# Dilated attention in a three-block network: token order set when queries and keys are evicted, values of two groups reordered through DRAM

## The chip, the cores and the metric

One core of a Trainium2 chip runs the whole program. The metric is the device time of one execution in microseconds. The kernel before was run three times: 3733.88, 3742.0 and 3743.15 us, median 3742.0 us.

## The reference

The network has three blocks of layers over 512 tokens of width 1024. The change lies in the second block, whose attention has twelve heads of 64 in three groups of four. Group 0 looks at neighbouring tokens in blocks of 128. Groups 1 and 2 are dilated by 4: token t belongs to sub-sequence t mod 4, and each of the four sub-sequences of 128 tokens attends only to itself. Cut to what matters, for one group:

```python
def to_sub(t):                       # dilation r, L = S // r
    return t.reshape(B, L, dilation, H, hd).transpose(0, 2, 3, 1, 4)
s = einsum('brhnqd,brhnkd->brhnqk', to_sub(q), windows(to_sub(k))) * hd ** -0.5
s = where(valid, s - slopes * dist, -inf)
p = exp(s - max(s));  l = sum(p)
o = einsum('brhnqk,brhnkd->brhnqd', p, windows(to_sub(v))) / l
```

The three groups are merged by their log-sum-exp. Everything is computed in float32.

## The kernel before

Activations lie with the features on the 128 partitions and the 512 tokens along the free dimension. A float32 product is made from three products of a high and a low part (`mm3`, line 253, and `gemm_tok`, lines 354 to 356): high by high, high by low, low by high. Weights arrive in tiles of 128 x 1024 (512 KB) on SP's queue (line 236) into three buffers `wraw`; ScalarE copies the high part (`whi`, line 369), VectorE takes the difference (`wlo`, line 370).

`gemm` computes features by tokens: the weight block is the stationary operand, the tokens move, 512 columns at a time. 24 matmuls make one output tile `pg`, of which there are two in PSUM, and an `evac` function empties it. `gemm_tok` computes tokens by features, for the values: the stationary operand is 128 tokens of the activations `h`, the weights move, and four output tiles (two `pg`, two `pa`) are filled in turn, 96 matmuls in all for a weight of up to 512 columns.

In the second block `b2_body` runs the product of the convolution branch (12 feature tiles), then `b2_attention`, then further products (`ev_sc` and on). `b2_attention` (line 1531) loops over the three groups. For each, `project(g)` computes two tiles of queries and two of keys with `gemm` and empties them on ScalarE (lines 1545 and 1547), computes the values with `gemm_tok` at 256 columns (line 1550, emptied on ScalarE), and four bias tiles on VectorE (line 1553). Then 16 units follow (`unit`, four blocks j by four heads): a score product (line 834, queries stationary, keys moving), a biased maximum on VectorE (line 837), an exponential on ScalarE (line 838), a transpose on TensorE (line 847), a copy on ScalarE (line 850) and the product with the values (line 854). In group 0 a unit has one or two key blocks (28 in 16 units); in groups 1 and 2 it has one.

The tokens of a dilated block j are every fourth token. `b2_sub` (line 1416) picks them by a view with a step of four elements:

```python
return ap.rearrange("p (l r) -> p r l", r=4)[:, j]
```

This view is used for the stationary tokens of the values of groups 1 and 2, and for both operands of their score products. `b2_merge` (line 1581) uses it again at the end.

Program order and priorities set the order on each engine; it is fixed when the kernel is built. The units belong to a second stream, so that TensorE gets the products of the next `project` between the steps of the units. The depthwise convolution of 31 taps (`b2_conv`, line 1510, VectorE) is emitted with a later priority and fills VectorE beside these stages. Tiles of `s4` (queries, keys, values, bias, outputs) come from 25 buffers; `tmp` of stream "d" has four buffers.

Of the kernel before, what the change touches and what calls it, by code (L numbers as in the profile page):

```python
# [10 lines left out]
F32 = mybir.dt.float32  # L11
# [3 lines left out]
AF = mybir.ActivationFunctionType  # L15
# [4 lines left out]
T = 512  # L20
# [30 lines left out]
class Core:  # L51
# [422 lines left out]
    def ffn(self, h, up, down, conv, end):  # L474


        nc = self.nc
        self.set_rows(h)
        hid = self.parts()
        held = {}  # L480

        def ev(m, ps):
            j = m // 2
            u = ps
            if conv is not None:
                u = self.tmp()
                self.conv_evac(u, ps, lambda i: conv(m * 3 + i), 3)
            if m % 2 == 0:
                s = self.tmp()
                nc.scalar.activation(s, u, AF.Silu)  # L490
                held[j] = s
            else:
                s = held.pop(j)
                nc.vector.tensor_mul(s, s, u)  # L494
                self.split(hid.hi(j), hid.lo(j), s)

        self.gemm(up, h, ev, wide=True)
        evac, after = end()
        self.gemm(down, hid, evac, tail=getattr(evac, "tail", 0))
        with self.stream("b"):  # L500
            return after()
# [911 lines left out]
class Block2:  # L1413


    def b2_sub(self, ap, g, j):
# [2 lines left out]
            return ap[:, j * 128 : j * 128 + 128]  # L1419
        return ap.rearrange("p (l r) -> p r l", r=4)[:, j]  # L1420

    def b2_mixer(self, h, end):
        with self.phase("b2", 25, dict(a=2, b=4, d=4)):
            return self.b2_body(h, end)
# [106 lines left out]
    def b2_attention(self, w, h, at):  # L1531
        nc, a = self.nc, self.a
        ml = self.small([128, 2, 3, 4, 4], tag="ml", bufs=1)
        nm, ls = ml[:, 0], ml[:, 1]
        ob, qs, ks, vs, bs, pos = [], [], [], [], [], {}

        def project(g):
            q, k, v, bias = self.s4(), self.s4(), self.s4([128, 4, 256]), self.s4([128, 4, 256])
            for l, t in ((qs, q), (ks, k), (vs, v), (bs, bias)):
                l.append(t)  # L1540

            def ev(m, ps):
                i = (m - 12) % 4
                if i < 2:
                    nc.scalar.activation(q[:, i], ps, AF.Copy, scale=0.125)
                else:
                    nc.scalar.activation(k[:, i - 2], ps, AF.Copy)

            self.gemm(w, h, ev, 12 + 4 * g, 4)
            self.gemm_tok(a["b2_v"], self.tok(h, lambda x, j: self.b2_sub(x, g, j)), lambda j, ps: nc.scalar.activation(v[:, j], ps, AF.Copy), g * 256, 256)  # L1550
            wd = 256 if g == 0 else 128
            for hd in range(4):
                nc.vector.tensor_scalar(bias[:, hd, :wd], self.c(f"d{g}"), -float(2.0 ** (-8.0 * (4 * g + hd + 1) / 12)), None, ALU.mult)

        def unit(g, j, hd):
            r = slice(hd % 2 * 64, hd % 2 * 64 + 64)
            q, k, v = qs[g][r, hd // 2], ks[g][r, hd // 2], vs[g]
            if g == 0:
                vb = max(j - 1, 0)
                k, bias = k[:, vb * 128 : (j + 1) * 128], bs[g][:, hd, 256 - 128 * (j + 1 - vb) : 256]  # L1560
            else:
                vb, k, bias = j, self.b2_sub(k, g, j), bs[g][:, hd, :128]
            wd = bias.shape[-1]
            p = self.attn_scores(self.b2_sub(q, g, j), k, wd, bias, ls[:, g, j, hd : hd + 1], m=nm[:, g, j, hd : hd + 1])
            yield
            if hd == 0:
                pos[g, j] = self.ps()
                if j == 0:
                    ob.append(self.s4([128, 4, 256]))
            self.attn_pv(pos[g, j][:, hd * 64 : hd * 64 + 64], p, wd, lambda b: v[:, vb + b, hd * 64 : hd * 64 + 64])  # L1570
            if hd == 3:
                nc.scalar.activation(ob[g][:, j], pos.pop((g, j))[:, :256], AF.Copy)

        for g in range(3):
            project(g)
            with self.stream("b"):
                self.pipeline(unit(g, j, hd) for j in range(4) for hd in range(4))
        with self.stream("b"):
            self.b2_merge(ob, nm, ls, at)
# [42 lines left out]
class Block3:  # L1622
# [47 lines left out]
    def b3_body(self, h, end):  # L1670
# [81 lines left out]
        rproj = lambda: proj("b3_rproj", 0, ry, parts)  # L1752
        work = [*qkv, *gates, zs, rproj]
        xs = [run(j, self.rwkv_in, w, h, j) for j in range(2)]
        for j in range(4):
            if 0 < j < 3:
                xs.append(run(j + 1, self.rwkv_in, w, h, j + 1))
            n = B3_FILL[j]
            fill(B3_PACE[j], work[:n])
            del work[:n]  # L1760
            run(j, self.rwkv, xs[j], j, lora, lt, gs, half, oka, ry)
# [371 lines left out]
class Net(Core, Layer0, Layer1, Block2, Block3):  # L2133
# [348 lines left out]
    def run(self, out):  # L2482
        nc, tc, a = self.nc, self.tc, self.a
        self.xd = self.ctx.enter_context(tc.tile_pool(name="xd", bufs=1, space=bass.MemoryType.DRAM)).tile([128, KD, T], F32, name="xd")
        self.gd = self.ctx.enter_context(tc.tile_pool(name="gd", bufs=1, space=bass.MemoryType.DRAM)).tile([128, 16, T], F32, name="gd")
        self.xin = a["xT"]
        self.mod = self.cpool.tile([128, 96], F32, name="mod")
        units = lambda layer, m0, m1: [lambda m=m: self.ada_bg(layer, m) for m in range(m0, m1, 2)]
        ada = [units(0, 16, 40), units(0, 40, 48) + units(1, 0, 40), [], units(1, 40, 48)]
        with self.psum(a=2, b=4):  # L2490
            with tc.tile_pool(name="ada", bufs=1) as self.apool:
                self.scb = self.apool.tile([128, D], F32, name="scb")
                with self.phase("x0", dict(s4=4, sq=2, wa0=WA0), dict(a=3), side="right"):
                    h = self.first_norm()

                for layer in range(2):
                    self.bg.extend(ada[2 * layer])
                    self.bg_per = 1
                    end = self.end_gated(layer, f"l{layer}_post_m", 2, self.ada_norm(f"l{layer}_pre_f", layer, 4, 3), TAIL[layer])
                    h = (self.l1_mixer if layer else self.l0_mixer)(h, end)  # L2500
                    self.bg_flush()
                    self.bg.extend(ada[2 * layer + 1])
                    self.bg_per = FBG
                    if layer == 0:
                        norm = self.ada_norm("l1_pre_m", 1, 1, 0)
                    else:
                        norm = lambda r, x, update, h, half: self.norm_h(r, x, lambda k: self.v("b2_g1", k), None, update, h, half)
                    with self.phase(f"ffn{layer}", 26, dict(d=3, b=2)):
                        h = self.ffn(h, a[f"l{layer}_up"], a[f"l{layer}_down"], None, self.end_gated(layer, f"l{layer}_post_f", 5, norm, TAIL[2 + layer], False))
                    self.bg_flush()  # L2510

            ffn = lambda n, h, end: self.ffn(h, a[f"b{n}_up"], a[f"b{n}_down"], lambda c: self.v(f"b{n}_fw", c), end)
            h = self.b2_mixer(h, self.end_add("b2_g2"))
            with self.phase("ffn2", 26, dict(d=6, b=3)):
                h = ffn(2, h, self.end_block)
        with self.psum(a=3, b=3):
            h = self.b3_mixer(h, self.end_add("b3_g2"))
            with self.phase("ffn3", 26, dict(d=6, b=3)):
                ffn(3, h, lambda: self.end_last(out))
# [23 lines left out]
```

## Time and profile before

| what | value |
|---|---|
| median of three runs | 3742.0 us |
| the profiled execution | 3741.21 us |
| its span in the trace | 3739.4 us |
| mean granted clock of TensorE | 0.975 of full speed |
| TensorE (PE) busy | 3637.7 us, 97% |
| weight loads into TensorE (PEld) | 2956.0 us, 79% |
| VectorE (DVE) busy | 2192.0 us, 59% |
| ScalarE (ACT) busy | 1357.4 us, 36% |

The span is what the trace covers; 1.8 us lie around it. PE is the matmul, PEld the load of the stationary operand, which can run beside the matmul before it. A busy PE says that matmuls were in flight, not that they ran at their best rate, so that the pitch of the matmuls (start to start) and the granted clock have to be read too.

### The profile page before, as it was taken

Reading aid. Unit: us, or ns where it says so; the run is one execution under the profiler, and the core shown is the slowest. Engines: PE = TensorE matmul, PEld = TensorE weight load, DVE = VectorE, ACT = ScalarE, POOL = GpSimd, SP = SyncE. Lnnn points to the kernel's source line nnn. Section 1 sums busy time; section 2 is a strip of 40 time slices with the busy share of each in tenths; the row PEclk is TensorE's granted clock in tenths of the full one; section 3 lists DMA queues with packets and bytes.
Section 4 is the critical chain, followed back from the end, with each engine's and each line's share of the span. In section 5 each row is a group of like instructions: output and inputs, shape, how many; then the busy total and the mean of one; then the engine's idle time right before and its main releaser. Section 6 shows DMA issues by size and latency. Waiting matters only on the chain.

```text
span 3739.4 us, 50867 instructions
## 1 busy us (share of the span) xinstructions
PE 3637.7 (97%) x20496; PEld 2956.0 (79%) x20496; DVE 2192.0 (59%) x3821; ACT 1357.4 (36%) x2197; POOL 242.1 (6%) x216
## 2 busy tenths in 40 slices
PE   6998999999999999999999999999999999999999
PEld 5776888878887788878888888788877777887887
DVE  7866665454377653349519354675466655766752
ACT  5444432334254432323332243443343332333432
POOL 2003100110021200100000010000000000100000
PEclk9999999999999999999979999999999999999999
DMA  6511265533300242323112234223321111052232
GB/s 216 184 46 62 98 208 193 167 108 101 122 28 23 68 158 96 118 90 110 51 40 74 86 103 138 96 96 119 110 83 42 62 63 44 27 186 86 98 116 78
DMA packets 120220, 373.56 MB, mean 100 GB/s; under 512 B 12064, under 2 KB 20256, under 8 KB 119984
## 3 DMA queue, kind: packets, MB, share of 16 engines
q1 hardware_dynamic: 105008, 322.05, 26.4%
q10 hardware_dynamic: 14976, 48.26, 3.8%
q8 instruction: 161, 2.64, 0.3%
q14 instruction: 75, 0.61, 0.1%
HBM read 349.29 MB, written 20.97 MB: 99 GB/s over the span
## 4 chain that ended last, share of the span: by engine, by line
PE 91%; DVE 6%; ACT 1%; issue 1%; DMA 0%; POOL 0%; POOLq 0%; DVEq 0%; ACTq 0%
PE pg L253 67%; PE pa L253 3%; PE pb L854 2%; PE pb L834 1%; PE pb L847 1%; PE pb L1274 1%; DVE wlo L370 1%; PE pa L392 1%; PE pg L1361 1%; PE pb L2275 1%; PE pg L354 1%; PE pa L354 1%; PE pa L355 1%; PE pg L356 1%; PE pg L355 1%
## 5 line engine op out<-in xcount | busy, mean ns | idle before, releaser
L253 PE MATMUL pg<-h,whi 128*128 128x512 f32 (+1 forms) x5584 | 1776.2, 397 | 45.4 <-ACT h L463 14.4
L253 PEld LDWEIGHTS pg<-h,whi 128*128 128x128 f32 x5584 | 1049.1, 191 | 278.2 <-issue 18.7
L253 PE MATMUL pg<-h,wlo 128*128 128x512 f32 (+1 forms) x2792 | 1101.2, 395 | 0.0
L369 ACT ACTIVATE whi<-wraw 128x1024 fp32r<-128x1024 f32 (+3 forms) x540 | 546.9, 1014 | 1351.0 <-PE pg L253 1062.8
L370 DVE TENSOR_TENSOR wlo<-wraw,whi 128x1024 fp32r<-128x1024 f32 (+3 forms) x540 | 638.9, 1184 | 638.6 <-ACT whi L369 636.0
L253 PE MATMUL pg<-s,whi 128*128 128x512 f32 (+1 forms) x2044 | 620.5, 386 | 3.4 <-DVE s L916 2.8
L253 PEld LDWEIGHTS pg<-h,wlo 128*128 128x128 f32 x2792 | 533.5, 191 | 109.7 <-issue 4.2
L253 PEld LDWEIGHTS pg<-s,whi 128*128 128x128 f32 x2044 | 379.9, 189 | 84.1 <-DVE s L916 3.2
L253 PE MATMUL pg<-s,wlo 128*128 128x512 f32 (+1 forms) x1022 | 392.7, 384 | 0.0
L253 PEld LDWEIGHTS pg<-s,wlo 128*128 128x128 f32 x1022 | 192.9, 189 | 38.0
L807 DVE SCALAR_TENSOR_TENSOR td<-td,vec,td 128x511 f32<-128x511 f32 (+1 forms) x188 | 139.9, 747 | 59.8 <-ACT td L803 58.2
L2153 DVE CUSTOM_DVE_ANT_0 wa<-wa,scb,vec 128x1024 f32<-128x1024 f32 x90 | 121.3, 1350 | 65.6 <-DMA wa<-in_l_ada_dram 65.5
L332 DVE TENSOR_TENSOR td<-pg,rows 128x512 f32<-128x512 f32 x130 | 89.3, 688 | 86.1 <-PE pg L253 85.6
L1510 DVE SCALAR_TENSOR_TENSOR s<-s,vec,s 128x504 f32<-128x504 f32 (+25 forms) x180 | 121.5, 731 | 0.4
L854 PEld LDWEIGHTS pb<-s,tb 128*128 128x128 f32 x600 | 86.3, 203 | 31.4 <-DVE tb L852 9.1
L369 ACT ACTIVATE s<-td 128x512 fp32r<-128x512 f32 x94 | 59.3, 631 | 106.8 <-DVE td L494 106.3
L253 PE MATMUL pa<-h,whi 128*128 128x512 f32 (+1 forms) x336 | 95.8, 359 | 0.0
L854 PE MATMUL pb<-s,tb 128*128 128x64 f32 x600 | 92.3, 284 | 3.2 <-DVE tb L852 3.2
L370 DVE TENSOR_TENSOR s<-td,s 128x512 fp32r<-128x512 f32 x94 | 66.9, 712 | 30.7 <-ACT s L369 30.7
L494 DVE TENSOR_TENSOR td<-td,pg 128x512 f32<-128x512 f32 x44 | 30.2, 687 | 75.9 <-PE pg L253 75.8
L253 PEld LDWEIGHTS pa<-h,whi 128*128 128x128 f32 x336 | 61.2, 194 | 8.9 <-issue 0.2
L803 ACT ACTIVATE td<-td,vec 128x512 f32<-128x512 f32 x94 | 66.5, 709 | 4.5 <-DVE td L332 3.1
(804 smaller groups left out, 4145.2 us busy)
## 6 DMA issues: line engine op xcount, KB each, us to landing
wraw<-in_b_in_dram SPq DMA_DIRECT2D x112, 512.0 KB, 3.2
wraw<-in_l_up_dram SPq DMA_DIRECT2D x88, 512.0 KB, 3.2
wraw<-in_b_up_dram SPq DMA_DIRECT2D x88, 512.0 KB, 3.2
wa<-in_l_ada_dram ACTq DMA_DIRECT2D x80, 512.0 KB, 3.2
wraw<-in_l_in_dram SPq DMA_DIRECT2D x51, 512.0 KB, 3.5
wraw<-in_l_down_dram SPq DMA_DIRECT2D x32, 512.0 KB, 3.5
wraw<-in_b_down_dram SPq DMA_DIRECT2D x32, 512.0 KB, 3.5
xd<-s SPq DMA_DIRECT2D x28, 512.0 KB, 2.7
```

The costliest lines, as they stand in the source:

```text
L253: mm = lambda *a, **k: self.nc.tensor.matmul(*a, **k, skip_group_check=True)
L332: self.nc.vector.tensor_mul(y, ps, rows)
L354: nc.tensor.matmul(pss[j][:, :n], xh, wh, start=k == 0, stop=False)
L355: nc.tensor.matmul(pss[j][:, :n], xl, wh, start=False, stop=False)
L356: nc.tensor.matmul(pss[j][:, :n], xh, wl, start=False, stop=k == nk - 1)
L369: i = nc.scalar.activation(hi, src, AF.Copy)
L370: nc.vector.tensor_sub(lo, src, hi.bitcast(F32))
L803: nc.scalar.activation(out, ps, AF.Copy, scale=w(taps - 1))
L807: nc.vector.scalar_tensor_tensor(out[:, s:], ps[:, : T - s], w(taps - 1 - s), out[:, s:], ALU.mult, ALU.add)
L854: nc.tensor.matmul(o, st[:, b * 128 : b * 128 + 128], v(b), start=b == 0, stop=b == nb - 1)
L1510: nc.vector.scalar_tensor_tensor(out[:, s:], x[:, : T - s], tap(30 - s), out[:, s:], ALU.mult, ALU.add)
L2153: nc.vector.tensor_tensor_reduce(w, w, self.scb, 1.0, b, ALU.mult, ALU.add, o)
```

## The change

The values of groups 1 and 2 are computed first, by one `gemm_tok` of 512 columns on the tokens in their natural order. Each of its four output tiles is copied by ScalarE into a `tmp` and written to a DRAM tile `vd` (two groups, 512 tokens, 256 columns), 256 KB at a time, on ScalarE's queue. `project(1)` and `project(2)` no longer compute values: they load their `v` tile from `vd` on SP's queue, 512 KB, so that partition l holds tokens 4l to 4l+3. Queries and keys of groups 1 and 2 are written in the order of the sub-sequences when they are emptied from PSUM: the read of PSUM has the step of four, the tile in SBUF is then contiguous for each block, and the score products read it without a step. Group 0 is as before.

```diff
+    def b2_values(self, h):
+        nc = self.nc
+        def ev(j, ps):
+            t = self.tmp()
+            nc.scalar.activation(t, ps, AF.Copy)
+            nc.scalar.dma_start(self.vd[:, j * 128 : j * 128 + 128].rearrange("g t n -> t g n"), t.rearrange("p (g n) -> p g n", g=2))
+        self.gemm_tok(self.a["b2_v"], self.tok(h), ev, 256, 512)
...
             def ev(m, ps):
                 i = (m - 12) % 4
-                if i < 2:
-                    nc.scalar.activation(q[:, i], ps, AF.Copy, scale=0.125)
-                else:
-                    nc.scalar.activation(k[:, i - 2], ps, AF.Copy)
+                o = (q, k)[i // 2][:, i % 2]
+                if g:
+                    o, ps = o.rearrange("p (r l) -> p r l", r=4), ps.rearrange("p (l r) -> p r l", r=4)
+                nc.scalar.activation(o, ps, AF.Copy, scale=1.0 if i // 2 else 0.125)
             self.gemm(w, h, ev, 12 + 4 * g, 4)
-            self.gemm_tok(a["b2_v"], self.tok(h, lambda x, j: self.b2_sub(x, g, j)), lambda j, ps: nc.scalar.activation(v[:, j], ps, AF.Copy), g * 256, 256)
+            if g:
+                nc.sync.dma_start(v, self.vd[g - 1].rearrange("(l r) n -> l r n", r=4))
+            else:
+                self.gemm_tok(a["b2_v"], self.tok(h), lambda j, ps: nc.scalar.activation(v[:, j], ps, AF.Copy), 0, 256)
...
-                vb, k, bias = j, self.b2_sub(k, g, j), bs[g][:, hd, :128]
+                vb, k, bias = j, k[:, j * 128 : j * 128 + 128], bs[g][:, hd, :128]
             wd = bias.shape[-1]
-            p = self.attn_scores(self.b2_sub(q, g, j), k, wd, bias, ls[:, g, j, hd : hd + 1], m=nm[:, g, j, hd : hd + 1])
+            p = self.attn_scores(q[:, j * 128 : j * 128 + 128], k, wd, bias, ls[:, g, j, hd : hd + 1], m=nm[:, g, j, hd : hd + 1])
...
+        self.b2_values(h)
         for g in range(3):
             project(g)
...
+        self.vd = self.ctx.enter_context(tc.tile_pool(name="vd", bufs=1, space=bass.MemoryType.DRAM)).tile([2, T, 256], F32, name="vd")
```

## Rows read from the trace of the kernel before

**Rows 1.** The page: busy time, and the chain that ended last, by engine.

```profile
PE 3637.7 (97%) x20496; PEld 2956.0 (79%) x20496; DVE 2192.0 (59%) x3821; ACT 1357.4 (36%) x2197; POOL 242.1 (6%) x216
...
PE 91%; DVE 6%; ACT 1%; issue 1%; DMA 0%; POOL 0%; POOLq 0%; DVEq 0%; ACTq 0%
```

**Rows 2.** Busy time by stretch: length, engines (counts), clock, DMA share, GB/s.

```profile
core 0: us, PE busy (x) PEld busy (x) DVE busy (x) ACT busy (x) POOL busy (x), PEclk, DMA share, GB/s
1400.00:1500.00 100.00, 100.00 (x443) 82.81 (x442) 33.83 (x37) 29.60 (x38) 0.00 (x0) 1.00 0.29 97
...
1773.20:1785.00 11.80, 11.80 (x98) 11.55 (x96) 11.80 (x20) 3.47 (x6) 0.00 (x0) 1.00 0.28 90
1785.00:1820.40 35.40, 35.40 (x181) 25.25 (x180) 28.62 (x65) 20.41 (x60) 0.00 (x0) 1.00 0.10 32
...
1827.90:1850.60 22.70, 22.70 (x99) 22.57 (x100) 3.00 (x6) 4.17 (x7) 0.00 (x0) 1.00 0.15 47
```

**Rows 3.** Timeline of PE: first and last of the 96 value matmuls, group 1.

```profile
1827.93 0.28 PE L354 MATMUL pg<-whi,h 128*128 128x256 f32 x1
...
1849.99 0.39 PE L356 MATMUL pa<-wlo,h 128*128 128x256 f32 x1
```

**Rows 4.** Line 355, values: weight loads (ns min/median/max) of groups 0 and 1.

```profile
L355 PEld LDWEIGHTS pg<-whi,h x16: 187/192/192, 1773.3 to 1783.9; 128*128 128x128 f32 x16
...
L355 PEld LDWEIGHTS pg<-whi,h x16: 310/329/329, 1827.9 to 1848.2; 128*128 128x128 f32 x16
```

**Rows 5.** Timeline of PE around a score product of groups 0 and 1.

```profile
1789.39 0.48 PE L834 MATMUL pb<-s,s 64*128 64x128 f32 x2
1789.81 0.33 PE L847 MATMUL pb<-cst,tb 128*128 128x128 f32 x1
...
1854.59 0.83 PE L834 MATMUL pb<-s,s 64*128 64x128 f32 x2
1855.35 0.50 PE L253 MATMUL pg<-h,wlo 128*128 128x512 f32 x1
```

**Rows 6.** Line 834, score products: weight loads of group 0, then of group 1.

```profile
L834 PEld LDWEIGHTS pb<-s,s x32: 182/184/186, 1785.1 to 1813.7; 64*128 64x128 f32 x32
...
L834 PEld LDWEIGHTS pb<-s,s x32: 304/316/328, 1850.3 to 1881.6; 64*128 64x128 f32 x32
```

**Rows 7.** Line 253 alone by stretch: length, PE, PEld (counts), clock, DMA share, GB/s.

```profile
1785.00:1820.40 35.40, 19.68 (x63) 10.84 (x64) 1.00 0.10 32
...
1850.60:1864.30 13.70, 6.37 (x19) 3.25 (x19) 1.00 0.12 39
1864.30:1887.80 23.50, 14.80 (x26) 7.77 (x27) 0.50 0.07 22
...
1922.20:1929.30 7.10, 3.42 (x11) 1.89 (x12) 1.00 0.23 74
1929.30:1960.30 31.00, 17.18 (x28) 8.40 (x28) 0.50 0.05 17
...
1980.00:1992.00 12.00, 10.19 (x24) 6.23 (x23) 0.57 0.28 89
```

**Rows 8.** Line 834 alone, start of group 1's attention: columns as in rows 7.

```profile
1850.70:1864.30 13.60, 6.14 (x18) 3.93 (x16) 1.00 0.12 40
```

**Rows 9.** Eviction of queries (line 1545), then copies without and with step.

```profile
L1545 ACT ACTIVATE s<-pg x6: 574/580/593, 1757.9 to 1889.9; 128x512 f32<-128x512 f32 x6
...
L1594 DVE COPY s<-pb x6: 673/1042/1081, 1960.6 to 1964.8; 4x512 f32<-4x512 f32 x6
```

**Rows 10.** DMA: issue on ScalarE's queue, then transfers through DRAM (us to landing).

```profile
L1718 ACTq DMA_DIRECT2D gd<-td x16: 326/326/336, 2951.7 to 3172.9; - x16
...
s<-xd SPq DMA_DIRECT2D x28, 512.0 KB, 6.0
...
gd<-td ACTq DMA_DIRECT2D x16, 256.0 KB, 2.3
```

**Rows 11.** Timeline of DVE: the last eviction of the product ahead of the attention.

```profile
1752.24 0.68 DVE L1439 TENSOR_TENSOR s<-td,pg 128x512 f32<-128x512 f32 x1
```

## The prediction

> **What bounds the kernel now.** I read the page first: TensorE is busy 97% of the span and carries 91% of the chain that ended last [rows 1], so time is won where TensorE's own work shrinks. But busy is not fast. In the table by stretch a plain 512-column product runs 443 matmuls in 100 us, a pitch of 0.226 us [rows 2]; this is the yardstick. The stretch of the values of group 1 is just as busy, yet it puts 96 matmuls of only 256 columns into 22.3 us (first to last 22.06 us over 95 steps, 0.232 us each) [rows 3]. In that stretch PEld is busy 22.57 of 22.70 us [rows 2]: the weight loads set the pace. They take 329 ns where they read every fourth token and 192 ns where they read neighbours [rows 4]. Third, the score products: a unit of 128 keys holds TensorE 0.76 us in group 1 and 0.42 us in group 0 [rows 5], with weight loads of 316 against 184 ns [rows 6]. Last, the granted clock, by stretch: it is 1.00 (2.4 GHz) throughout the attention of group 0, but falls to 0.50 (1.2 GHz) after 13.7 us in that of group 1 and after 7.1 us in that of group 2, and stays there for 23.5 and 31.0 us [rows 7]. TensorE was never idle there; what differs from group 0 is the stepped operands and one key block per unit instead of up to two.
>
> **The values.** Removed: two stretches like the one in rows 3, 2 x 96 x 0.232 = 44.5 us, all on TensorE, with nothing else in flight. Added: one product of 96 matmuls of 512 columns on neighbouring tokens. Its weight loads are the 192 ns kind and hide behind a 512-column matmul, so the pitch is the yardstick's: 96 x 0.226 = 21.7 us. **Gain 22.8 us.** The weight bytes are the same, six tiles of 512 KB.
>
> The Trainium skill (SBUF — State Buffer, Specifications (TRN2), row on cachelines) says that SBUF reads are fast when at least two hits fall into a 16-byte line, so that a step of four float32 pays on every element. By that rule the contiguous load runs at its full rate; the 329 against 192 ns above agree in direction, and the sum uses the rows alone.
>
> **The scores.** 32 units of groups 1 and 2 lose 0.76 - 0.42 = 0.34 us each, 10.9 us if the clock is full.
>
> **The clock.** I count it together with the scores, from whole stretches. Attention of group 1 lasts 13.7 + 23.5 = 37.2 us and holds 45 plain matmuls (10.2 us at the yardstick), so its 16 units cost 27.0 us. Group 2 lasts 38.1 us with 39 plain matmuls (8.8 us): 29.3 us. Together 56.3 us for 32 units [rows 7]. Group 0 at full clock: 35.4 us less 63 x 0.226 = 14.2 leaves 21.2 us for 16 units of 28 key blocks, 1.32 us a unit, 0.76 us a block. A contiguous unit of one block at full clock should cost about that 0.76 us. A check from today's full-clock stretch: 13.7 us less 19 x 0.226 leaves 9.4 us, with 9 pairs of score matmuls [rows 7, 8], 1.04 us a unit, less 0.34 is 0.70; the last units were unfinished there, so it is a lower end. The upper end is 1.32, if the chain of VectorE and ScalarE in a unit, not TensorE, sets the pace. I take 0.76, since the plain matmuls between the steps cover that chain in group 0 although VectorE is 81% busy there [rows 2]. 32 x 0.76 = 24.3 us: **gain 32.0 us**, of which 10.9 are the scores and 21.1 the clock. It rests on the clock staying at 2.4 GHz as in group 0.
>
> **What is counted at nothing.** Evictions of queries and keys with the step on the PSUM side: 8 of them. The trace has no ScalarE read with a step; the nearest row is a VectorE copy, 673 ns without and 1081 ns with a step (there on the SBUF side) [rows 9]. So 580 ns become between 580 and 930 ns, 2.8 us of ScalarE at most in all. A `pg` tile is emptied while the other takes 24 matmuls, 5.4 us, which covers it; without that cover it would cost TensorE the 2.8 us. A gain is excluded, since the same bytes are read. The four new evictions of 512 columns with a DMA issue behind each (580 + 326 ns, 3.6 us together [rows 9, 10]) replace eight of 256 columns; behind them on ScalarE stand the next weight splits and the first query eviction. The three `wraw` tiles ahead (3 x 5.4 us) cover the splits; the cost without cover would be 3.6 us. The four `tmp` buffers wait for their writes, 2.3 us each [rows 10], and nobody takes one before the units of group 0.
>
> SP gets two more instructions. Each 512 KB load waits for the four writes of `vd`, done over 60 us before the first unit of group 1 (21.7 us of queries and keys, 11.8 us of values and 35.4 us of attention of group 0 lie between [rows 2]), and lands in about 6 us [rows 10]; weight loads queue behind it, again under the 16 us of tiles ahead. The new product starts where the convolution branch ends and needs the second `pg` tile about nine matmuls (2 us) after its first. VectorE empties that tile in 0.68 us [rows 11], behind whatever convolution step or weight split stands ahead of it: no wait, or under 1 us. The product of group 0's values and the merge are as they were. VectorE's convolution gets 21.7 us more beside plain matmuls before the first unit; that helps if anything.
>
> **The sum.** The profiled execution took 3741.2 us, 0.8 below the median of the runs. 3741.2 - 22.8 - 32.0 = 3686.4; I give 3687, nothing being added for the small terms.
>
> **The rivals.**
> *The clock falls anyway* (a unit of one block may be too thin whatever its step). Then 14 units at full clock gain 0.34 us (4.8 us), and 18 at half clock gain between 0.13 (if the contiguous score grows from 0.42 to 0.63) and 0.34, say 4 us. With the values that is 32 us: 3709; if one of the two groups holds, 3698. For it speaks that the fall came only in groups of one block; against it, that both fallen stretches are just those with the step, and that the stretch of rows 3 with its 256-column matmuls kept 1.00.
> *The units are bound by their chain*, 1.32 us each: 42.2 us instead of 24.3, a gain of 14.1 from the attention, 3704.
> *Stepped reads of PSUM hold up TensorE's writes.* 8 evictions of up to 0.93 us, in which matmuls run at half rate, cost at most 7.4 us: 3694. The Trainium skill (PSUM — Partial Sum Buffer, Specifications (TRN2), row on cachelines) says of PSUM that any non-contiguous access significantly slows matmuls; no row here shows a stepped PSUM read, so this stays possible.
> *Slower: SP's queue stands still.* If the load of `v` is placed early on SP and its `s4` buffer is still occupied, every weight load waits behind it. Beyond 16 us TensorE starves. Held from the end of the new product to the end of group 0's attention it would stand those 69 us, 53 us lost; twice, for both loads, 106 us, less the 55 gained: 3792. It decides from a stand of about 80 us in all. Against it: up to the outputs of group 2 I count 20 of 25 `s4` buffers in use, so no load has to wait for one.
>
> **How the numbers follow.** Clock holds and units run at 0.76 us: 0.56, 3687. Clock falls wholly or in one group: 0.20. Chain-bound units: 0.13. PSUM: 0.05. SP: 0.03. The remaining 0.03 is a mix in which small losses eat the gain to within 0.3%, about what a measurement of this kernel can tell from no change. All but the last two are over 0.3% faster: 0.94. The range reaches up to the fallen clock, 3711. Downward: units at 0.70 give 2 us, and the third stretch at low clock, in the merge (12.0 us at 0.57, 24 plain matmuls [rows 7]), could recover up to 5 us if the denser attention carries the clock over; the lowest run shown lies 8 us under the median. 3677.
>
> **What would show it.** In the changed profile: 96 value matmuls of 512 columns at a pitch of 0.226 us ahead of the first queries, with weight loads of about 190 ns; no value stretch between the queries of a group and its units; score pairs at 0.42 us with loads of 184 ns; granted clock 1.00 from there to the end of group 2's units; query evictions of groups 1 and 2 between 580 and 930 ns with no idle time of TensorE behind them. The forecast is wrong if the clock is at 0.50 in those units, if TensorE waits for the copies of the transposes, or if it waits for weight splits after a load of `v`.

## The result, and the profile after

The changed kernel takes 3687.94 us (median of four runs, 3687.85 to 3689.53) against 3742.57 us for the kernel before (also four runs now, 3733.88 to 3750.65): ratio 0.9855, 95% interval 0.984 to 0.987. The forecast was 3687 us, with a range of 3677 to 3711. The profiled execution took 3687.85 us, its span is 3686.0 us, 53.4 us shorter than that of before. The total was met. Of the two gains that it was added up from, that of the values was met and that of the attention was not, as the parts below show.

The page of the changed kernel, busy time and chain by engine, answers to [rows 1]:

```profile
PE 3587.1 (97%) x20400; PEld 2907.2 (79%) x20400; DVE 2192.0 (59%) x3821; ACT 1356.2 (37%) x2193; POOL 242.7 (7%) x216
...
PE 91%; DVE 6%; ACT 1%; issue 1%; POOL 0%; DMA 0%; POOLq 0%; DVEq 0%; ACTq 0%
```

PE lost 50.6 us and 96 matmuls; VectorE and ScalarE are as busy as they were. The chain is still TensorE's, so the time came out of its own work. The timeline of PE around the new product (the last row is the first matmul of the queries) answers to [rows 3]:

```profile
1752.84 0.39 PE L354 MATMUL pg<-whi,h 128*128 128x512 f32 x1
...
1774.61 0.39 PE L356 MATMUL pa<-wlo,h 128*128 128x512 f32 x1
1774.84 0.61 PE L253 MATMUL pg<-h,whi 128*128 128x512 f32 x2
```

96 matmuls in 22.0 us, a pitch of 0.229 us against a forecast of 0.226. Weight loads, the evictions of queries and keys (line 1559) and the copies of the new product (line 1429), from the views of lines 355, 834, 1559 and 1429 of the changed kernel, answer to [rows 4, 6, 9] (line 834 over all three groups, group 0 included):

```profile
L355 PEld LDWEIGHTS pg<-whi,h x16: 187/188/189, 1752.8 to 1772.8; 128*128 128x128 f32 x16
L834 PEld LDWEIGHTS pb<-s,s x96: 182/184/186, 1808.4 to 1909.5; 64*128 64x128 f32 x96
L1559 ACT ACTIVATE s<-pg x12: 576/580/598, 1781.2 to 1889.1; 128x512 f32<-128x512 f32 x12
L1429 ACT ACTIVATE td<-pg x2: 598/599/600, 1773.0 to 1774.1; 128x512 f32<-128x512 f32 x2
```

No load of these two lines takes over 189 ns. Of the twelve evictions on line 1559, eight read PSUM with the step, and all take 576 to 598 ns: the stepped read costs nothing. The score products, on the timeline of group 1, answer to [rows 5]. A pair is the two matmuls of one score product (x2 in the row); from pair to transpose it is 0.42 us instead of 0.76.

```profile
1854.39 0.48 PE L834 MATMUL pb<-s,s 64*128 64x128 f32 x2
1854.81 0.33 PE L847 MATMUL pb<-cst,tb 128*128 128x128 f32 x1
1855.06 0.48 PE L834 MATMUL pb<-s,s 64*128 64x128 f32 x2
```

The plain products (line 253) by stretch, with the granted clock, answer to [rows 7]: attention of groups 0, 1 and 2, then the stretch at low clock in the merge.

```profile
1808.50:1841.40 32.90, 17.01 (x53) 9.13 (x54) 1.00 0.10 33
1851.50:1875.70 24.20, 14.37 (x43) 7.24 (x43) 1.00 0.14 44
1888.30:1912.60 24.30, 13.45 (x40) 6.76 (x39) 1.00 0.13 45
1931.00:1946.00 15.00, 11.82 (x25) 7.66 (x25) 0.56 0.20 70
```

The clock is full in both attentions. Worked as the prediction worked it, the units of group 1 take 24.2 - 43 x 0.226 = 14.5 us, 0.91 us each, those of group 2 24.3 - 40 x 0.226 = 15.3 us, 0.95 us each; the forecast was 0.76.

**Where the time went.** Two marks stand in every version and cut the span into three pieces: M1 is the one VectorE eviction of a `pa` tile in the convolution branch's product, well before anything that the change touches; M2 is the first transpose of the merge. Their rows in the first profile of the kernel before, then in that of the changed kernel:

```profile
L1439 DVE TENSOR_TENSOR s<-td,pa x1: 678/678/678, 1710.5 to 1710.5; 128x512 f32<-128x512 f32 x1
L1590 PE MATMUL pb<-cst,mla x24: 271/273/300, 1960.0 to 1962.9; 128*4 128x128 f32 x24
...
L1451 DVE TENSOR_TENSOR s<-td,pa x1: 681/681/681, 1711.9 to 1711.9; 128x512 f32<-128x512 f32 x1
L1606 PE MATMUL pb<-cst,mla x24: 272/272/273, 1911.6 to 1914.6; 128*4 128x128 f32 x24
```

and in the second profile of the kernel before ("before, again" below):

```profile
L1439 DVE TENSOR_TENSOR s<-td,pa x1: 680/680/680, 1722.8 to 1722.8; 128x512 f32<-128x512 f32 x1
...
L1590 PE MATMUL pb<-cst,mla x24: 272/273/273, 1955.0 to 1958.0; 128*4 128x128 f32 x24
```

For every profiled execution (the last two columns are the time at low clock, a granted clock of about 0.5, inside the attentions of groups 1 and 2, read from the granted clock in slices of 3 us):

| profiled execution | start to M1 | M1 to M2 | M2 to end | span | low clock, group 1 | group 2 |
|---|---|---|---|---|---|---|
| before, first | 1710.5 | 249.5 | 1779.4 | 3739.4 | 24 us | 31 us |
| before, fourth | 1711.0 | 249.4 | 1786.3 | 3746.7 | 24 | 31 |
| before, third | 1720.4 | 242.9 | 1775.9 | 3739.2 | 3 | 34 |
| before, again | 1722.8 | 232.2 | 1773.8 | 3728.8 | none | none |
| order alone | 1717.8 | 222.0 | 1776.3 | 3716.1 | none | none |
| queries stepped | 1721.2 | 218.9 | 1781.7 | 3721.8 | 34 | none |
| values alone | 1711.4 | 211.2 | 1768.3 | 3690.9 | 3 | none |
| values unstepped in place | 1712.3 | 211.1 | 1768.4 | 3691.8 | none | none |
| keys stepped | 1712.8 | 206.1 | 1781.7 | 3700.6 | none | none |
| one product, no DRAM | 1713.5 | 200.7 | 1773.6 | 3687.8 | none | none |
| step on the write | 1711.9 | 200.5 | 1776.1 | 3688.5 | none | none |
| after, again | 1710.8 | 199.7 | 1774.4 | 3684.9 | none | none |
| after, first | 1711.9 | 199.7 | 1774.4 | 3686.0 | none | none |

Only the middle piece holds the change. Between the first profiles it shrank by 49.8 us; of the 53.4 us of the span, 5.0 came behind M2 and -1.4 before M1, where the code is the same and one kernel's executions differ by 12.3 us before M1 and 12.5 us behind M2 on their own. Behind M2 that spread is the low clock again: added up from the granted clock, the first profile of before has 52.3 us of it there and that of the changed kernel 41.9, and in all thirteen executions the length of this piece less half of its low-clock time lies between 1751.6 and 1754.4 us. The middle piece splits by the fourth row: 249.5 - 232.2 = **17.3 us are the low clock**, which the kernel before pays in some executions and not in others, and 232.2 - 199.7 = **32.5 us are work**: the values 22.6 (two stretches of 22.3 us against one of 22.0; the 22.2 in expectations below runs to the end of the last matmul), the rest 9.9.

54.6 us at half clock cost 17.3 us and not 27, in the main because a pair with both operands stepped takes 0.76 us at either clock (18 such pairs, 13.7 us, lie wholly in it). From the fallen stretch of group 1 in the first profile, where one plain product after another took 0.43 us from start to start:

```profile
1873.16 0.83 PE L834 MATMUL pb<-s,s 64*128 64x128 f32 x2
1873.92 1.22 PE L253 MATMUL pg<-h,whi 128*128 128x512 f32 x2
```

### The profile page after: what moved, and what is told of

It is laid out like the page before. It is cut to its first block, busy times and chain, and to the rows that moved or that the text cites. A ratio compares the mean times of both kernels' runs of the same rounds, so it can differ in the third digit from the quotient of the medians.

```text
span 3686.0 us, 50689 instructions
## 1 busy us (share of the span) xinstructions
PE 3587.1 (97%) x20400; PEld 2907.2 (79%) x20400; DVE 2192.0 (59%) x3821; ACT 1356.2 (37%) x2193; POOL 242.7 (7%) x216
## 4 chain that ended last, share of the span: by engine, by line
PE 91%; DVE 6%; ACT 1%; issue 1%; POOL 0%; DMA 0%; POOLq 0%; DVEq 0%; ACTq 0%
PE pg L253 68%; PE pa L253 3%; PE pb L854 2%; PE pb L834 1%; PE pb L847 1%; PE pb L1274 1%; DVE wlo L370 1%; PE pa L392 1%; PE pg L1361 1%; PE pb L2291 1%; DVE wa L2169 0%; PE pb L1967 0%; PE pa L1068 0%; PE pg L354 0%; PE pa L426 0%
## 5 line engine op out<-in xcount | busy, mean ns | idle before, releaser
L253 PEld LDWEIGHTS pg<-h,whi 128*128 128x128 f32 x5584 | 1047.0, 190 | 277.0 <-ACT h L463 18.8
L1522 DVE SCALAR_TENSOR_TENSOR s<-s,vec,s 128x493 f32<-128x493 f32 (+25 forms) x180 | 120.5, 731 | 0.2
L494 DVE TENSOR_TENSOR td<-td,pg 128x512 f32<-128x512 f32 x44 | 30.2, 687 | 75.8 <-PE pg L253 75.8
```

Of the source, the lines that this page charges most:

```text
L253: mm = lambda *a, **k: self.nc.tensor.matmul(*a, **k, skip_group_check=True)
L1522: nc.vector.scalar_tensor_tensor(out[:, s:], x[:, : T - s], tap(30 - s), out[:, s:], ALU.mult, ALU.add)
```

## The experiments

In the first four, against the kernel before at 3734.42 us on that chip (eight runs, 3731.8 to 3738.34), one part of the change is done or undone alone.

**Values alone.** The changed kernel with the scores of before: queries and keys in natural order, both operands stepped.

```diff
-                if g:
-                    o, ps = o.rearrange("p (r l) -> p r l", r=4), ps.rearrange("p (l r) -> p r l", r=4)
-                vb, k, bias = j, k[:, j * 128 : j * 128 + 128], bs[g][:, hd, :128]
+                vb, k, bias = j, self.b2_sub(k, g, j), bs[g][:, hd, :128]
-            p = self.attn_scores(q[:, j * 128 : j * 128 + 128], k, wd, bias, ls[:, g, j, hd : hd + 1], m=nm[:, g, j, hd : hd + 1])
+            p = self.attn_scores(self.b2_sub(q, g, j), k, wd, bias, ls[:, g, j, hd : hd + 1], m=nm[:, g, j, hd : hd + 1])
```

> The values of groups 1 and 2 come from one product and go through DRAM as in the change; queries and keys keep the natural order, so the score products read both with the step. Theory (the step in the score products takes the clock down): only the value term is won, 44.6 - 22.2 = 22.4 us, so about 3720 us; the granted clock is again 0.50 in most of the attention of groups 1 and 2, and a score pair there takes 0.76 us. Rival (the stretch of stepped weight loads right ahead of each attention is what lets the clock fall later): the clock stays at 1.00 in both attentions and the time is about 3707 us.

Measured: 3694.95 us (3692.7 to 3703.0), ratio 0.990, interval 0.9884 to 0.9917. The timeline of PE shows the stepped pair as before, 0.76 us:

```profile
1854.29 0.83 PE L834 MATMUL pb<-s,s 64*128 64x128 f32 x2
1855.05 0.33 PE L847 MATMUL pb<-cst,tb 128*128 128x128 f32 x1
```

M1 to M2 is 211.2 us, 11.5 more than in the changed kernel; the step on 32 pairs at 0.34 us is 10.9. So stepped scores cost their own time, and the clock fell for some 3 us only, not for the 54 us of rows 7. That the step in the score products brings the low clock every time, on which the clock term of the prediction rested, falls here. The span of this execution is only 4.9 us longer than that of the changed kernel because the piece behind M2, alike in code, came out 6.1 us shorter, with 30.2 us at low clock in it instead of 41.9.

**Order alone.** The values as before, the scores as in the changed kernel.

```diff
-            if g:
-                nc.sync.dma_start(v, self.vd[g - 1].rearrange("(l r) n -> l r n", r=4))
-            else:
-                self.gemm_tok(a["b2_v"], self.tok(h), lambda j, ps: nc.scalar.activation(v[:, j], ps, AF.Copy), 0, 256)
+            self.gemm_tok(a["b2_v"], self.tok(h, lambda x, j: self.b2_sub(x, g, j)), lambda j, ps: nc.scalar.activation(v[:, j], ps, AF.Copy), g * 256, 256)
-        self.b2_values(h)
```

> Queries and keys are put in the groups' order when evicted; the values are computed per group with stepped weight loads as in the kernel before. Theory: the value term stays, the attention term is won, 26 us by the two traces, so about 3716 us, with a granted clock of 1.00 in both attentions and 22.3 us for each value stretch. Rival (the stepped value stretches bring the clock down): the clock falls to 0.50 in the attentions, only 32 x 0.34 us at most are won, and the time is about 3732 us.

Measured: 3719.51 us (3712.39 to 3722.04), ratio 0.9956, interval 0.9941 to 0.9971. M1 to M2 is 222.0 us, 22.3 above the changed kernel; the values' 44.6 - 22.0 is 22.6 us. No low clock in the attentions.

**Keys stepped** and **queries stepped.** The changed kernel with one of the two left in natural order and read with the step (the second diff likewise, with `i >= 2` and the view on `q`).

```diff
-                if g:
+                if g and i < 2:
-                vb, k, bias = j, k[:, j * 128 : j * 128 + 128], bs[g][:, hd, :128]
+                vb, k, bias = j, self.b2_sub(k, g, j), bs[g][:, hd, :128]
```

> As the change, but the keys keep their natural order, so that only the moving operand of the score products of groups 1 and 2 has the step. Theory (the weight load is what costs: 316 against 184 ns in the traces): score pairs stay near 0.42 us, the clock stays at 1.00, about 3688 us. Rival (the moving operand is what costs): pairs near 0.76 us, the clock falls in groups 1 and 2, about 3715 us. In between if each has a part.

> As the change, but the queries keep their natural order, so that only the stationary operand of the score products of groups 1 and 2 has the step. Theory (the weight load is what costs): loads of 316 ns, pairs near 0.76 us, the clock falls to 0.50 in groups 1 and 2, about 3715 us. Rival (the moving operand costs): pairs near 0.42 us, clock 1.00, about 3688 us. In between if each has a part.

Measured: 3702.73 us (3695.34 to 3704.74), ratio 0.991, interval 0.9896 to 0.9925, with the keys stepped; 3701.69 us (3698.95 to 3723.54, five runs), ratio 0.9925, interval 0.9901 to 0.9949, with the queries stepped. One pair on the timeline of PE, keys stepped (moving operand):

```profile
1855.57 0.70 PE L834 MATMUL pb<-s,s 64*128 64x128 f32 x2
1856.20 0.33 PE L847 MATMUL pb<-cst,tb 128*128 128x128 f32 x1
```

and queries stepped (stationary operand):

```profile
1863.98 0.73 PE L834 MATMUL pb<-s,s 64*128 64x128 f32 x2
1864.64 0.33 PE L847 MATMUL pb<-cst,tb 128*128 128x128 f32 x1
```

Pairs of 0.63 and 0.66 us, between 0.42 with none and 0.76 with both stepped: each operand has its own price, 0.21 and 0.24, and together they cost less than the sum (0.34). With the keys stepped M1 to M2 grew by 6.4 us, against 32 x 0.21 = 6.7. The profiled execution with stepped queries was the longest of its five, 3723.54 us, and the low clock is a part of the reason: 34 us of group 1, with no stretch of values anywhere near. Against the profile with the keys stepped it is 12.8 us longer from M1 to M2 and 8.4 us before M1. Plain products by stretch in it, group 1 from its fall on, then group 2:

```profile
1867.00:1901.00 34.00, 20.00 (x34) 10.40 (x35) 0.50 0.04 16
1916.00:1938.00 22.00, 9.92 (x27) 4.79 (x27) 1.00 0.14 49
```

Of the next seven, four (both kernels again, one product without DRAM, values unstepped) were run against the kernel before at 3743.86 us on another chip (15 runs, 3724.7 to 3749.79), and three (before for the third and fourth time, step on the write) against 3743.61 us on a third chip (seven runs, 3742.39 to 3745.91).

**Before, again**, and **after, again.** Both kernels unchanged.

> The kernel before, unchanged, profiled a second time. Theory (the fall of the granted clock in the attentions of groups 1 and 2 is not the same in every execution): its runs on the other chip lay between 3732 and 3738 us, 3 to 9 us under the first profile, so the clock should be at 0.50 for less than the first profile's 54 us there. Rival (it falls alike each time, and the runs differ elsewhere): again about 54 us at 0.50 in the two attentions.

> The changed kernel, unchanged, beside the kernel before on one chip. Theory: no stretch of it lies near the point where the clock falls, but for the merge, so its runs stay within about 2 us of each other around 3688 us, and the gain over the kernel before on this chip is 46 to 55 us, as the latter's own time goes.

Measured: before 3740.34 us (3730.56 to 3752.94, eight runs), ratio 1.0002, interval 0.9982 to 1.0021; after 3688.53 us (3686.3 to 3692.5, five runs), ratio 0.9864, interval 0.9837 to 0.9892. Eight runs of the kernel before spread over 22 us, five of the changed one over 6. The profiled execution of before was its shortest, 3730.56 us, and the clock never fell in its attentions (line 253, group 1's later part and group 2):

```profile
1871.00:1892.00 21.00, 10.54 (x30) 5.26 (x31) 1.00 0.07 25
1925.00:1956.00 31.00, 13.46 (x39) 6.74 (x39) 1.00 0.10 34
```

**Before, third and fourth.** One more profiled execution each, to see whether longer executions are those with the fall.

> The kernel before, unchanged, one more look. Theory (in the kernel before the clock falls in the attentions of groups 1 and 2 in some executions and not in others, and that is most of its spread): the part from the end of the convolution branch to the first merge transposes lasts about 193 us where the clock holds and up to 209 us where it falls to 0.50 in both; an execution above 3740 us shows the fall, one below 3733 us shows none. Rival (the fall in the first profile was a rare event and the spread comes from elsewhere): no fall in the attentions whatever the time, and the part lasts 193 us.

> The kernel before, unchanged, a third look beside the second, with the same expectations: 193 us from the end of the convolution branch to the first merge transposes without a fall, up to 209 us with one, and the time above 3740 us only with one; by the rival no fall whatever the time.

Measured: 3740.93 us and 3748.47 us. Line 253 in the third profile of before, group 1 up to its brief dip, then group 2:

```profile
1857.00:1879.00 22.00, 8.13 (x24) 4.18 (x24) 1.00 0.08 25
1932.00:1966.00 34.00, 17.16 (x28) 8.44 (x28) 0.51 0.05 16
```

In the fourth, group 1 and group 2:

```profile
1864.50:1888.00 23.50, 14.51 (x25) 7.62 (x26) 0.51 0.06 22
1929.50:1960.50 31.00, 17.17 (x28) 8.45 (x28) 0.50 0.05 17
```

All three profiled executions above 3740 us show the fall, the one below 3733 us does not, and M1 to M2 is 249.5, 249.4, 242.9 and 232.2 us in the order of the low clock (the expectations count from a mark some 40 us later). The rival of a rare event falls. But the fall is worth 17 us at most; the rest of the spread is in the other two pieces, which the change does not touch. With only four profiles of before, the share of executions that fall is not settled.

**One product, no DRAM.** The one product of 512 columns runs on the stepped tokens and is emptied straight into the `v` tiles of both groups, since both use the same order; `vd`, its writes and loads are gone.

```diff
-            t = self.tmp()
-            nc.scalar.activation(t, ps, AF.Copy)
-            nc.scalar.dma_start(self.vd[:, j * 128 : j * 128 + 128].rearrange("g t n -> t g n"), t.rearrange("p (g n) -> p g n", g=2))
-        self.gemm_tok(self.a["b2_v"], self.tok(h), ev, 256, 512)
+            for g in range(2):
+                nc.scalar.activation(vs[g][:, j], ps[:, g * 256 : g * 256 + 256], AF.Copy)
+        self.gemm_tok(self.a["b2_v"], self.tok(h, lambda x, j: self.b2_sub(x, 1, j)), ev, 256, 512)
```

> As the change, but the one product of the values of groups 1 and 2 takes the tokens with the step (both groups have the same step), so that its output is already in the groups' order: ScalarE writes it straight into the two value tiles, eight copies of 256 columns (385 ns each), and the way through DRAM falls away. Theory (a 512-column matmul covers a stepped weight load of 329 ns as far as the 0.232 us pitch of the stepped value stretch): 96 x 0.232 = 22.3 us for the product against 22.2 us in the change, the DRAM trip was hidden, so the same time within 2 us. Rival (the load is not covered at 512 columns, about 0.33 us a matmul): 32 us, 10 us slower than the change. Second rival (the stepped loads let the clock fall after it): 10 to 20 us slower, with 0.50 in an attention.

Measured: 3689.56 us (3689.09 to 3690.47), ratio 0.9865, interval 0.9838 to 0.9892: the changed kernel's time. Weight loads and last matmuls of the product (lines 355 and 356), then its first matmuls on the timeline of PE:

```profile
L355 PEld LDWEIGHTS pg<-whi,h x16: 310/310/329, 1754.5 to 1775.2; 128*128 128x128 f32 x16
...
L356 PE MATMUL pa<-wlo,h x16: 387/394/401, 1755.7 to 1777.1; 128*128 128x512 f32 x16
```

```profile
1754.51 0.40 PE L354 MATMUL pg<-whi,h 128*128 128x512 f32 x1
1754.75 0.39 PE L355 MATMUL pg<-whi,h 128*128 128x512 f32 x1
```

The loads are stepped and slow, 310 to 329 ns, yet the pitch is 0.238 us against 0.229 (1754.51 to 1777.1 over 95 steps; 0.9 us over 96 matmuls): the same loads that gave 256-column matmuls their pitch of 0.232 now bring twice the columns each. **Doubling the columns is enough for the gain of the values; the contiguous load adds under 1 us to it**, and the trip through DRAM wins nothing here; it costs nothing either.

**Values unstepped in place.** The kernel before with the value products of groups 1 and 2 on neighbouring tokens, so that the reordering of the values is left out.

```diff
-            self.gemm_tok(a["b2_v"], self.tok(h, lambda x, j: self.b2_sub(x, g, j)), lambda j, ps: nc.scalar.activation(v[:, j], ps, AF.Copy), g * 256, 256)
+            self.gemm_tok(a["b2_v"], self.tok(h), lambda j, ps: nc.scalar.activation(v[:, j], ps, AF.Copy), g * 256, 256)
```

> The kernel before, but the values of groups 1 and 2 are computed in place on the tokens in natural order, 256 columns, so that the reordering of the values is left out; the score products keep the step. Theory (a stepped value stretch ahead of a stepped attention is what the clock falls after): value stretches of 11.5 instead of 22.3 us, 21.6 us won, and the clock held in the attentions, up to 20 us more: 3735 - 21.6 - 20 = about 3694 us on the other chip's level. Rival (the step in the scores alone does it, and the first profile of the values-only kernel was a lucky one): 21.6 us won, about 3713 us, clock at 0.50 in the attentions.

Measured: 3695.19 us (3691.8 to 3698.91), ratio 0.988, interval 0.9852 to 0.9908. M1 to M2 is 211.1 us, 0.1 from the values alone. Weight loads and last matmuls of group 1's values:

```profile
L355 PEld LDWEIGHTS pg<-whi,h x16: 187/192/192, 1829.7 to 1840.3; 128*128 128x128 f32 x16
...
L356 PE MATMUL pa<-wlo,h x16: 279/283/283, 1830.3 to 1841.3; 128*128 128x256 f32 x16
```

From the first matmul at 1829.68 that is a pitch of 0.122 us, so that two products of 256 columns with fast loads take 23.5 us against 22.0 for one of 512 columns. Either cure, unstepped loads or wider matmuls, is enough by itself, to within 1.5 us. The scores are stepped here and the clock held, in the one execution that was profiled.

**Step on the write.** The changed kernel with the step of the evictions moved from the read of PSUM to the write in SBUF. It is not the same step there: PSUM is read in order, and neighbouring elements are written 128 elements apart.

```diff
-                    o, ps = o.rearrange("p (r l) -> p r l", r=4), ps.rearrange("p (l r) -> p r l", r=4)
+                    o, ps = o.rearrange("p (r l) -> p l r", r=4), ps.rearrange("p (l r) -> p l r", r=4)
```

> The changed kernel with the step of the query and key evictions moved from the read of PSUM to the write in SBUF (PSUM is read in order, the tile is written with the step). Theory: the eviction is covered wherever the step is, so the time is the changed kernel's, 3688 us within 3, ratio 0.986; if a stepped SBUF write costs ScalarE, it shows as an eviction of up to 930 ns instead of 580 (the ratio of the VectorE copies, 1081 to 673) and still costs nothing. Rival (the step is only free on the PSUM side and evictions hold up the products): 8 x 0.35 us, 3691 us.

Measured: 3690.07 us (3688.18 to 3697.56), ratio 0.9862, interval 0.9845 to 0.9878; M1 to M2 0.8 us longer. The view of line 1559 (eight of the twelve are stepped):

```profile
L1559 ACT ACTIVATE s<-pg x12: 577/1082/1112, 1781.3 to 1889.5; 128x512 f32<-128x512 f32 x12
```

The same copy costs ScalarE 580 ns with the step of four on the PSUM side and about 1090 with the step of 128 on the SBUF side, more than the 930 expected from [rows 9], where the step of the write was four. TensorE hardly notices: 8 x 0.5 = 4 us of ScalarE left 0.8 us in the middle piece.

## Why the prediction came true, point by point

- **The values: right, and priced right.** Forecast 22.8 us, measured 22.6; the order alone, which lacks just this part, is 22.3 us behind in M1 to M2. Of the two reasons given, the fast load and the cover of the wider matmul, either suffices: the version without DRAM has only the wider matmul, the values unstepped in place have only the fast load.
- **The scores: right.** 32 x 0.34 = 10.9 us forecast; 11.5 us in the values alone, 9.9 as the rest of the work. Added up from start to start, the pairs of the two groups take 22.7 us in the second profile of before and 12.5 in the changed kernel, 10.2 less.
- **The clock: the term was too large, and its cause was wrong.** From attention the prediction took 56.3 - 24.3 = 32.0 us, 21.1 of it clock. By the same reckoning 56.3 - 29.8 = 26.5 us came (49.8 - 22.6 = 27.2 between the marks, which also take in what lies between the windows). Two steps failed. First, "A contiguous unit of one block at full clock should cost about that 0.76 us" divided by blocks what goes in part by units. The timeline of the changed kernel shows a unit of two blocks in group 0, then one of a single block in group 1 (its next rows stand with the result above):

```profile
1820.48 0.44 PE L847 MATMUL pb<-cst,tb 128*128 128x128 f32 x2
1820.85 0.70 PE L834 MATMUL pb<-s,s 64*128 64x256 f32 x2
1821.48 0.50 PE L253 MATMUL pg<-h,wlo 128*128 128x512 f32 x1
1821.81 0.55 PE L854 MATMUL pb<-s,tb 128*128 128x64 f32 x4
1822.17 0.49 PE L253 MATMUL pg<-h,whi 128*128 128x512 f32 x1
...
1854.03 0.43 PE L854 MATMUL pb<-s,tb 128*128 128x64 f32 x2
1854.39 0.48 PE L834 MATMUL pb<-s,s 64*128 64x128 f32 x2
```

  Start to start, transposes, scores and products with the values take 0.37 + 0.63 + 0.36 = 1.36 us for two blocks and 0.25 + 0.42 + 0.36 = 1.03 us for one. These are single units, and dear ones. Added up from start to start over the whole stretch, the 16 units of group 0 (28 blocks) take 18.8 us, 0.67 a block, and the 16 of group 1 12.1 us, 0.76 each: TensorE's own time for a unit happens to be the forecast's. But the plain products that stand among the units take 0.27 us in group 0 and 0.29 in group 1 from start to start, not the yardstick's 0.226, and the reckoning puts the difference on the units. It is 2.3 us in group 0 and 2.7 in group 1, 0.14 and 0.17 us a unit: it does not shrink when a unit has one block instead of 1.75 on average. 0.76 + 0.17 = 0.93 is the unit as measured. Why these plain products are slower at full clock is not shown. Second, the fall of the clock was taken as a fixed cost of the kernel before, from one execution, and tied to the step. It is worth 17.3, 17.2, 10.7 and 0 us in four executions (M1 to M2 less 232.2). All five executions in which it came have stepped score operands, and none of the five with ordered ones shows it; but three with the step, whole or in one operand, have none. The step goes with the fall, in these few executions, and does not settle it. Neither a value stretch ahead nor idle time is needed: with the queries stepped there is no such stretch, and TensorE was never idle in the falls of [rows 7]. What decides in one execution stays open.
- **Small terms counted at nothing: right.** The PSUM step measured 0 ns, and the DMAs through `vd` are hidden. Issue of the writes (line 1430) and of the loads (line 1563) of the changed kernel:

```profile
L1430 ACTq DMA_DIRECT2D vd<-td x4: 366/382/453, 1773.6 to 1776.4; - x4
...
L1563 SPq DMA_DIRECT2D s<-vd x2: 418/422/425, 1841.9 to 1879.9; - x2
```

  The loads land at most 4.6 us after their issue, at about 1846.5 and 1884.5, 5.0 and 3.8 us before the stretches of units that read them begin (1851.5 and 1888.3): covered, with that much to spare. What the weight loads into TensorE waited for, from the new product to the merge (us in total, times, longest):

```profile
PEld pb L854 <- ACT tb L850: 5.5, 16, 0.5
PEld pb L834 <- issue: 3.9, 16, 0.4
PEld pg L253 <- issue: 1.7, 5, 0.3
...
PEld pg L354 <- DVE s L1451: 0.4, 1, 0.4
...
PEld pg L354 <- ACT s L1559: 0.2, 1, 0.2
```

  The first row is a sign of being wrong that the prediction named: weight loads waited for the copies of the transposes, 1.8 or 1.9 us in each of the three attentions, as in that of group 0 before (1.7 us). How much of the 2.7 us above comes from that is not shown, since a weight load can run beside the matmul before it. The forecast start wait of "under 1 us" is the 0.4 us behind line 1451. No plain product waits for a weight tile, so however long SP's queue stood, it did not reach TensorE (the rival at 3792), and one wait of 0.2 us is all that stands behind an eviction of queries or keys.
- **The other rivals.** "The clock falls anyway" fell: 1.00 in both attentions of all five executions with ordered scores. "Units bound by their chain" at 1.32 us fell: they take 0.91 to 0.95. "Stepped reads of PSUM hold up TensorE" fell: the stepped reads take 576 to 598 ns, and between the attentions of groups 1 and 2 (1875.7 to 1888.3), where such evictions run, 55 plain matmuls stand in 12.6 us, 0.229 each. The Trainium skill (PSUM — Partial Sum Buffer, Specifications (TRN2), row on cachelines) says that any non-contiguous access significantly slows matmuls; for these reads by ScalarE the trace does not agree.
- **Why the total fits.** Middle piece 49.8 instead of 54.8, and 5.0 us that came behind M2. Those are not the change's: they are half of 10.4 us less of low clock in code that is alike, and the kernel before had 1773.8 us there in another execution, less than the changed one. The forecast of the total owes that much to luck. The merge's low-clock stretch, allowed for with a recovery of up to 5 us, stayed (15.0 us at 0.56).

## What to carry to other kernels

Where weight loads set the pace, either give each load more columns or make the load faster: here each alone brought nearly the whole gain, and one wide product on stepped tokens did as much as a trip through DRAM. Put an unavoidable step where ScalarE reads PSUM, where it cost nothing here, and not on the SBUF operands of TensorE, where it cost 0.34 us a score pair. A low clock seen in one profile is not a fixed cost: take a second and third execution, cut the span at marks that both kernels have, and charge to a change only what happens between them.

## What the runs showed of the hardware that was not expected

- A ScalarE copy of 128 x 512 float32 from PSUM to SBUF costs 580 ns with a step of four elements on the PSUM read and about 1090 ns with a step of 128 elements on the SBUF write.
- The same unchanged kernel runs two attention stretches at 2.4 GHz throughout in one execution (granted clock 1.00) and 54 us of them at 1.2 GHz (0.50) in another, with TensorE busy throughout.
- A score pair with both operands stepped takes 0.76 us at a granted clock of 0.50 as at 1.00, while a plain 512-column product goes from 0.23 to 0.43 us (kernel before, first and second profile).
- A stepped SBUF operand costs a score pair 0.21 us as the moving and 0.24 us as the stationary one, 0.34 us as both.
- A stepped weight load of 310 to 329 ns beside 512-column matmuls raises their pitch only from 0.229 to 0.238 us.
